# An eighth up-projection group in seven products, and low parts formed by accumulating DMAs

## The chip, the cores and the metric

The kernel runs on one core of one Trainium2 chip. The core has TensorE (PE in the profile, with PEld for its weight loads), VectorE (DVE), ScalarE (ACT), GpSimd (POOL) and SyncE (SP); SP and POOL issue the DMAs here. Each engine works through its own list of instructions in order and waits on semaphores of the others. The metric is the device time of one execution in microseconds (us); lower is better.

## The reference

Two layers of an encoder over 512 tokens with 1024 channels. Each layer has four mixing branches (a convolution module, neighbourhood attention, dilated attention, windowed attention) behind one input projection, merged by gates and projected back; then a ConvFFN:

```python
def _conv_ffn(h, w_up, conv_w, conv_b, w_down):
    u = _depthwise_conv(h @ w_up, conv_w, conv_b)
    gate, up = jnp.split(u, 2, axis=-1)
    return (jax.nn.silu(gate) * up) @ w_down
...
        x = x + mixed @ w_out[l]

        x = x + _conv_ffn(_rmsnorm(x, g_ffn[l]), w_up[l], ffn_conv_w[l], ffn_conv_b[l], w_down[l])
```

All is float32. `w_up` is 1024 x 5632 (2816 gate columns and 2816 up columns), `w_down` is 2816 x 1024, the depthwise convolution has width 3 along the tokens. The change lies in the ConvFFN alone.

## The kernel before

**Precision.** TensorE multiplies float32r, a float32 rounded to fewer bits. Each operand is split into a high part, hi = round(w), and a low part, lo = w - hi, and a product is three matmuls: hi x hi, hi x lo, lo x hi (L294 to L296, `prod`). So each weight tile of 128 x 1024 is loaded by SP into `w_raw` (L269), copied to `w_hi` by ACT (L273), and subtracted into `w_lo` by DVE (L275). A list, `w_list`, holds the weights of the whole program in the order of their use; `weights` emits each two units ahead of its use and with a high priority. `w_raw` has two buffers, `w_hi` and `w_lo` have three, so the parts of one unit can be written once TensorE has finished the unit three places earlier.

**Up-projection.** The 5632 columns are 44 blocks of 128: for i = 0 to 21 a gate block (s = 0) and an up block (s = 1). A block is 8 inner steps of three matmuls over all 512 tokens, 24 matmuls of 512 columns (`block`). Two neighbouring i make a group of four blocks; there are 11 groups. Groups 1 to 7 (`SEVEN`) are not made block by block. Each is one 2 x 2 block product (rows: gate and up; columns: the two halves of the 512 tokens; inner: even and odd steps of 128 channels) done by Winograd's scheme with seven products in place of eight: A11, S3, A22, S2, A12, S1, S4. One product is a unit of 24 matmuls of 256 columns (`seven`, L1128). The token side of the sums is formed once a layer (`ffn_form`). The weight side of the sums is formed in the raw tile: four quarters are loaded (L1270), and after the split of one unit a DMA from POOL's queue adds the next quarter onto the same tile (`grow`, L1258), which makes the next unit's weights. Each of these units is split into hi and lo by ACT (L1276) and DVE (L1277). Three of the seven results are copied out of PSUM by ACT (`sv`, L1140) and combined by DVE (L1143, L1147, L1152).

The list `UP_STEPS` sets the order: group 0 whole, then the units of the seven groups interleaved so that one group starts while the last one ends, then groups 8, 9 and 10 whole. Two blocks of the first whole group after them are drawn forward between the last units of seven products and kept in PSUM ("held" and "free").

**After each block.** DVE scales the result out of PSUM into a padded tile `U` (L1215, or L1144 to L1159 for seven products), which frees the PSUM bank. `conv_part` does the convolution in one ACT and two DVE operations (L1171 to L1173), ACT the silu for the gate half (L1177), DVE the product for the up half (L1185), which gives the activations f, kept two blocks to a tile of 128 x 1024.

**Down-projection.** It is a Winograd product as well, over 11 pairs of f blocks. Before its products a pair (f_i, f_k) has to become operands: DVE takes four sums of 256 columns (L1357, L1358, L1359, L1363), and f_i, f_k, the a-sums and the b-sum are each split into hi (ACT) and lo (DVE) at L1354 and L1355 (`split_pair`). Six pairs are split during the up-projection, after blocks 15 to 20 (`EARLY`), the five others in the first loop of `down`. The low parts are put into the tile of the f pair before (`pair_tags`), which is no longer needed then. The first products of `down` (L1376 to L1378) take four PSUM banks of the tag `mm`, which the last up blocks have used.

DVE, ACT and PE get their instructions in an order that a scheduler sets when the program is built, from the order of the code and its priorities.

Of the kernel before, what the change touches and what calls it, by code (L numbers as in the profile page):

```python
# [22 lines left out]
P = 128  # L23
L = 2
D = 1024
S = 512
KT = D // P
NB = S // P
DFF = 2816
# [3 lines left out]

CHUNK = 4

SEVEN = (1, 2, 3, 4, 5, 6, 7)


def up_steps():

    whole = lambda g: [('whole', 2 * g + i, s) for i in range(2) for s in range(2)]
    slots = {}
    for i, g in enumerate(SEVEN):
        for n, at in (('A11', 0), ('S3', 4), ('A22', 6), ('S2', 8), ('A12', 9), ('S1', 10), ('S4', 12)):
# [16 lines left out]
              ('gb', 'A22'), ('ga', 'S2'), ('ga', 'S1'), ('gb', 'S2'), ('gb', 'S1'), ('ga', 'S4'), ('gb', 'S4')]  # L61
MIX = (0, 1, 4, 5, 2, 3, 6, 7)

EARLY = (15, 16, 17, 18, 19, 20)
EPS = 1e-6
BIG = 1e30
EB = 4
# [167 lines left out]
class Trunk:  # L235
# [7 lines left out]
    def weights(self, upto, ahead=3000, parts=1, queue=None):  # L243

        nc = self.nc
        while self.w_emitted < min(upto, len(self.w_list)):
            n, pieces = self.w_list[self.w_emitted]
            if n == 'seven':
                with self.tc.high_priority(offset=ahead):
                    self.w_ready.append(self.seven_unit(*pieces))  # L250
                self.w_emitted += 1
                continue
            with self.tc.high_priority(offset=ahead):

                self.w_fast = (self.w_fast + 1) % 4 if n == 0 else 0
                if n == 0 and self.w_fast in (3, 0):
                    raw = self.fp.tile([P, 1024], F32, name="w_raw", tag="w_more", bufs=2)
                else:
                    raw = self.wpool.tile([P, 1024], F32, name="w_raw", tag="w_raw", bufs=2)
                hi = self.wpool.tile([P, 1024], F32R, name="w_hi", tag="w_hi", bufs=3)  # L260
                lo = self.wpool.tile([P, 1024], F32R, name="w_lo", tag="w_lo", bufs=3)
                src = pieces()
                n = sum(p.shape[1] for p in src)
                if len(src) == 1:
                    cut = [slice(i * n // parts, (i + 1) * n // parts) for i in range(parts)]
                    src = [src[0][:, s] for s in cut]
                c = 0
                for p in src:
                    (queue or nc.sync).dma_start(raw[:, c:c + p.shape[1]], p)  # L269
                    c += p.shape[1]  # L270
                for i in range(parts):
                    s = slice(i * n // parts, (i + 1) * n // parts)
                    w = nc.scalar.activation(hi[:, s], raw[:, s], AF.Copy)  # L273
                    self.first_hi = self.first_hi or w
                    nc.vector.tensor_tensor(lo[:, s], raw[:, s], hi[:, s].bitcast(F32), ALU.subtract)  # L275
            self.w_ready.append((hi, lo))
            self.w_emitted += 1

# [884 lines left out]
    def conv_part(self, i, s):  # L1163

        nc = self.nc
        v = nc.vector
        c = i + s * NF
        u = self.U[s][:, i % 2]
        y = self.fp.tile([P, S], F32, name=f"cy{s}", tag=f"cy{s}", bufs=2)
        w = lambda t: self.par('ffn_conv_w', c * 3 + t)  # L1170
        nc.scalar.activation(y, u[:, 1:513], AF.Identity, scale=w(1), bias=self.par('ffn_conv_b', c))  # L1171
        v.scalar_tensor_tensor(y, u[:, 0:512], w(0), y, ALU.mult, ALU.add)
        v.scalar_tensor_tensor(y, u[:, 2:514], w(2), y, ALU.mult, ALU.add)  # L1173

        if s == 0:
            si = self.fp.tile([P, S], F32, name="fth", tag="fth", bufs=2)
            nc.scalar.activation(si, y, AF.Silu)  # L1177
            self.silus[i] = si
            return
        if self.last and i % 2 == 1 and i // 2 < KT:  # L1180
            self.turn_res(i // 2)
        if i % 2 == 0:
            self.fpair = self.fp.tile([P, 1024], F32, name="f", tag=f"fp{i // 2}", bufs=1)
        fl = self.fpair[:, i % 2 * S:(i % 2 + 1) * S]
        v.tensor_tensor(fl, y, self.silus.pop(i), ALU.mult)  # L1185
        self.F.append(fl)
        if i in EARLY:
            self.split_pair(self.F, EARLY.index(i), self.got)

    def ffn(self, l, last):  # L1190
        nc = self.nc
        v = nc.vector
        self.U = []
        for i in range(2):
            u = self.conv_tile(f"U{i}")
            nc.gpsimd.memset(u[:, :, 0:1], 0.0)
            nc.gpsimd.memset(u[:, :, 513:514], 0.0)
            self.U.append(u)
        self.F, self.got, self.silus, self.sevens, self.last = [], {}, {}, {}, last
        held = {}  # L1200
        self.pace = 0.0
        for kind, a, b in UP_STEPS:
            if kind == 'seven':
                self.seven(a, b)
                continue
            if kind == 'free':
                ps = held.pop((a, b))
            else:
                ps = self.mm()
                self.block(ps)  # L1210
                self.tick()
            if kind == 'held':
                held[a, b] = ps
            else:
                v.tensor_tensor(self.U[b][:, a % 2, 1:513], ps, self.RB, ALU.mult)  # L1215
                self.conv_part(a, b)
        for g in self.slow:
            for _ in g:
                pass
        self.slow = []  # L1220
        return self.F
# [107 lines left out]
    def split_pair(self, F, j, got):  # L1329

        nc = self.nc
        v = nc.vector
        fi, fk = F[2 * j:2 * j + 2]

        def tile(t):
            if isinstance(t, tuple):
                t, n = t
                if n == 0:
                    pool = self.fp2 if t[:2] == "lt" else self.fp
                    self.halves[t] = pool.tile([P, 1024], F32R, name=f"p{t}", tag=t, bufs=1)  # L1340
                return self.halves[t][:, n * S:(n + 1) * S]
            pool = self.xpool if t[:2] in ("xh", "xl") else self.fp2 if t[:2] in ("fh", "t2", "t3") else self.fp
            return pool.tile([P, S], F32R, name=f"p{t}", tag=t, bufs=2 if t in ("lo", "xr", "xn", "cy0", "cy1") else 1)

        tags = self.pair_tags(j)
        ih, kh, il, kl, ah, al = (tile(t) for t in tags[:6])
        if j % 2 == 0:
            got['b'] = [tile(t) for t in tags[6:]]
        lo, hi = slice(0, 256), slice(256, 512)
        bh, bl = (t[:, (lo, hi)[j % 2]] for t in got['b'])  # L1350
        a = self.fp.tile([P, S], F32, name="sum", tag="xr" if j < len(EARLY) else "fth", bufs=2)

        def split(h, l, x):
            nc.scalar.activation(h, x, AF.Copy)  # L1354
            v.tensor_tensor(l, x, h.bitcast(F32), ALU.subtract)  # L1355

        v.tensor_tensor(a[:, lo], fi[:, hi], fk[:, hi], ALU.subtract)  # L1357
        v.tensor_tensor(fi[:, hi], fi[:, lo], fi[:, hi], ALU.subtract)  # L1358
        v.tensor_tensor(a[:, hi], a[:, lo], fi[:, lo], ALU.subtract)  # L1359
        split(ih, il, fi)  # L1360
        split(ah, al, a)
        split(kh, kl, fk)
        v.tensor_tensor(fk[:, lo], fk[:, lo], a[:, hi], ALU.add)  # L1363
        split(bh, bl, fk[:, lo])
        cut = lambda h, l, c: [(h[:, c + b * P:c + (b + 1) * P], l[:, c + b * P:c + (b + 1) * P]) for b in range(2)]
        got[j] = {'a11': cut(ih, il, 0), 's1': cut(ih, il, 256), 'a12': cut(kh, kl, 0), 's4': cut(kh, kl, 256),
                  's3': cut(ah, al, 0), 's2': cut(ah, al, 256), 'a22': cut(bh, bl, 0)}
# [108 lines left out]
    def run(self):  # L1476
        nc, tc = self.nc, self.tc
        with ExitStack() as st:
            pool = lambda name, **k: st.enter_context(tc.tile_pool(name=name, bufs=1, **k))
# [9 lines left out]
            for l in range(L):  # L1489
                off, quads, quarters, ups, mixing = 0, [], {}, {}, []  # L1490
                for kind, a, n in UNITS:
                    src = self.W[l, off:off + n * P].rearrange("(p c) -> p c", p=P)
# [16 lines left out]
                for kind, a, b in UP_STEPS:  # L1509
                    if kind == 'seven':  # L1510
                        self.w_list.append((kind, (l, a, b)))
                    elif kind != 'free':
                        self.w_list.append((1024, lambda src=ups[b * DFF + a * P]: [src]))
                self.quarters.append(quarters)
                self.quads.append(quads)
                self.sums.append([])
# [12 lines left out]
            with tc.tile_pool(name="first", bufs=1, reuse_waits="tile") as first:  # L1529
# [181 lines left out]
```

## Time and profile before

| | |
|---|---|
| three runs | 1549.47, 1544.78, 1548.46 us; median 1548.46 |
| the profiled execution, its own time | 1549.1 us |
| its span, first to last instruction | 1547.3 us |
| granted TensorE clock | 1.00 throughout |
| busy share of the span | PE 99%, PEld 86%, DVE 85%, ACT 62%, POOL 12% |
| DMA | 277.57 MB, 179 GB/s on average |
| layer 0: seven products, whole blocks, down-projection | about 447 to 610 us, 610 to 664 us, 664 to 760 us |
| layer 1: the same | about 1214 to 1382 us, 1382 to 1436 us, 1436 to 1530 us |

The busy time of an engine is the time in which at least one of its instructions ran. Matmuls overlap each other in TensorE's pipeline, so the cost of one is read from start to start. In a group of instructions, "out<-in" are the names of the tiles, then come the shapes, the count, the busy time of all, the mean duration of one in ns, and the idle time of the engine just before them with what ended it. Registers, branches and the issuing of DMAs don't count as busy. A wait names the instruction that waited and the one whose end released it. For a DMA the profile gives the time from its issue to its landing.

### The profile page before, as it was taken

To read this page: it belongs to the slowest core of one execution; us is meant where nothing else is said; L and a number is where in the kernel's file an instruction comes from. 1 tells how busy PE (TensorE), PEld (TensorE's weight loads), DVE (VectorE), ACT (ScalarE), POOL (GpSimd) and SP (SyncE) were. 2 spreads that over 40 slices of the span, in tenths; PEclk is the share of its full clock that TensorE was granted. 3 is DMA by queue.
4 is the path that set the end of the run, shared out by engine and by line. 5 is a ranking of instruction groups with operands and counts; after the bars stand their busy time and mean duration, and the time that the engine had idled before them with its cause. 6 is when DMAs were issued, how large, how long until landed. Compare 5 with 4: busy or idle time off the path is not lost.

```text
span 1547.3 us, 23306 instructions
## 1 busy us (share of the span) xinstructions
PE 1530.9 (99%) x8446; PEld 1325.7 (86%) x8446; DVE 1308.3 (85%) x2220; ACT 953.0 (62%) x1600; POOL 185.9 (12%) x280
## 2 busy tenths in 40 slices
PE   9999999999999999999999999999999999999998
PEld 8888888889889998878888888888898899998787
DVE  6689988797879989996576899887988789999974
ACT  6677777356655666564548687673566565665643
POOL 0123002220001110000002130023200011100000
PEclk9999999999999999999999999999999999999999
DMA  7789586756558886366558796866665699863664
GB/s 233 235 224 200 164 177 157 177 153 152 177 142 179 190 169 159 95 209 198 180 184 254 206 197 175 170 160 182 147 152 177 171 216 213 173 164 95 188 223 157
DMA packets 116739, 277.57 MB, mean 179 GB/s; under 512 B 27280, under 2 KB 29200, under 8 KB 116624
## 3 DMA queue, kind: packets, MB, share of 16 engines
q1 hardware_dynamic: 86800, 186.93, 37.7%
q0 software_dynamic: 29536, 88.62, 31.1%
q8 instruction: 67, 1.10, 0.3%
q10 hardware_dynamic: 288, 0.52, 0.1%
q14 instruction: 48, 0.39, 0.1%
HBM read 258.20 MB, written 58.72 MB: 205 GB/s over the span
## 4 chain that ended last, share of the span: by engine, by line
PE 69%; DVE 16%; DMA 6%; ACT 5%; issue 4%; SPq 0%; POOL 0%; ACTq 0%; DVEq 0%; POOLq 0%
PE mm L294 11%; PE mm L295 11%; PE mm L296 11%; PE aux L1128 5%; DVE w_lo L1277 4%; DMA chain<-W 4%; PE aux L948 3%; PE aux L1378 3%; PE aux L1377 3%; PE aux L1376 3%; DVE w_lo L275 2%; PE mm L1376 2%; PE mm L1378 2%; PE mm L1377 2%; DMA w_raw<-W 2%
## 5 line engine op out<-in xcount | busy, mean ns | idle before, releaser
L273 ACT ACTIVATE w_hi<-w_raw 128x1024 fp32r<-128x1024 f32 (+1 forms) x233 | 241.9, 1041 | 198.1 <-PE aux L1378 51.0
L275 DVE TENSOR_TENSOR w_lo<-w_raw,w_hi 128x1024 fp32r<-128x1024 f32 (+1 forms) x233 | 280.5, 1206 | 72.5 <-ACT w_hi L273 71.3
L294 PE MATMUL mm<-xh,w_hi 128*128 128x512 f32 x704 | 275.6, 391 | 0.0
L295 PE MATMUL mm<-xl,w_hi 128*128 128x512 f32 x704 | 274.6, 390 | 0.0
L296 PE MATMUL mm<-xh,w_lo 128*128 128x512 f32 x704 | 274.5, 390 | 0.0
L1128 PE MATMUL aux<-form,w_hi 128*128 128x256 f32 x896 | 160.8, 280 | 0.7 <-ACT sv L1140 0.7
L296 PEld LDWEIGHTS mm<-xh,w_lo 128*128 128x128 f32 x704 | 132.2, 188 | 28.3
L294 PEld LDWEIGHTS mm<-xh,w_hi 128*128 128x128 f32 x704 | 132.2, 188 | 26.3
L295 PEld LDWEIGHTS mm<-xl,w_hi 128*128 128x128 f32 x704 | 132.3, 188 | 25.9
L1128 PEld LDWEIGHTS aux<-form,w_hi 128*128 128x128 f32 x896 | 137.5, 188 | 1.7 <-ACT sv L1140 1.1
L1128 PE MATMUL aux<-form,w_lo 128*128 128x256 f32 x448 | 125.9, 281 | 0.0
L1277 DVE TENSOR_TENSOR w_lo<-chain,w_hi 128x1024 fp32r<-128x1024 f32 x72 | 87.9, 1220 | 32.2 <-ACT w_hi L1276 28.6
L1276 ACT ACTIVATE w_hi<-chain 128x1024 fp32r<-128x1024 f32 x72 | 76.0, 1056 | 61.4 <-DMA chain<-W 27.8
L469 DVE SCALAR_TENSOR_TENSOR cv<-cv,prm 128x512 f32<-128x512 f32 x120 | 94.7, 789 | 0.7
L1171 ACT ACTIVATE cy<-U,prm 128x512 f32<-128x512 f32 x88 | 67.9, 808 | 40.6 <-DVE U L1215 30.3
L1258 POOL DMA_DIRECT2D chain<-W x54 | 47.3, 876 | 328.9 <-DVE w_lo L1277 296.8
L1128 PEld LDWEIGHTS aux<-form,w_lo 128*128 128x128 f32 x448 | 84.1, 188 | 0.4 <-DVE w_lo L1277 0.4
L1276 ACT ACTIVATE w_hi<-w_raw 128x1024 fp32r<-128x1024 f32 x54 | 56.7, 1054 | 43.8 <-PE aux L1128 18.2
L532 PE MATMUL mm<-w_hi,xh 128*128 128x512 f32 x192 | 76.4, 398 | 0.3 <-DVE V L660 0.3
L533 PE MATMUL mm<-w_lo,xh 128*128 128x512 f32 x192 | 74.9, 390 | 0.0
L534 PE MATMUL mm<-w_hi,xl 128*128 128x512 f32 x192 | 74.9, 391 | 0.0
L1277 DVE TENSOR_TENSOR w_lo<-w_raw,w_hi 128x1024 fp32r<-128x1024 f32 x54 | 65.8, 1219 | 6.0 <-ACT w_hi L1276 4.6
(372 smaller groups left out, 3900.2 us busy)
## 6 DMA issues: line engine op xcount, KB each, us to landing
w_raw<-W SPq DMA_DIRECT2D x187, 512.0 KB, 4.4
chain<-W POOLq DMA_DIRECT2D x54, 512.0 KB, 5.7
sums<-W POOLq DMA_DIRECT2D x24, 1024.0 KB, 12.0
w_raw<-W SPq DMA_DIRECT2D x66, 256.0 KB, 3.8
w_raw<-sums SPq DMA_DIRECT2D x44, 256.0 KB, 3.8
w_raw<-sums SPq DMA_DIRECT2D x22, 512.0 KB, 4.3
sums<-W POOLq DMA_DIRECT2D x12, 768.0 KB, 10.3
chain<-W SPq DMA_DIRECT2D x18, 512.0 KB, 5.0
```

The costliest lines, as they stand in the source:

```text
L273: w = nc.scalar.activation(hi[:, s], raw[:, s], AF.Copy)
L275: nc.vector.tensor_tensor(lo[:, s], raw[:, s], hi[:, s].bitcast(F32), ALU.subtract)
L294: mm(ps, lhsT=wh, rhs=xh, start=start, stop=False)
L295: mm(ps, lhsT=wh, rhs=xl, start=False, stop=False)
L296: self.last_mm = mm(ps, lhsT=wl, rhs=xh, start=False, stop=stop)
L469: self.after_mm(v.scalar_tensor_tensor(acc, u[:, t:t + S], w(t), acc, ALU.mult, ALU.add))
L1128: self.last_mm = nc.tensor.matmul(o, lhsT=w[:, s], rhs=x, start=start and not (e or j or i), stop=j == 3 and i == 2, skip_group_check=True)
L1276: nc.scalar.activation(hi, raw, AF.Copy)
L1277: nc.vector.tensor_tensor(lo, raw, hi.bitcast(F32), ALU.subtract)
L1376: mm(ps, lhsT=x[0], rhs=w[0][:, cols], start=start, stop=False, skip_group_check=again)
L1377: mm(ps, lhsT=x[0], rhs=w[1][:, cols], start=False, stop=False, skip_group_check=again)
L1378: self.last_mm = mm(ps, lhsT=x[1], rhs=w[0][:, cols], start=False, stop=stop, skip_group_check=again)
```

## The change

**One more group in seven products.** `SEVEN` gets group 8. In each layer four whole blocks (16 and 17, gate and up) become seven units, and the held blocks are now those of block 18. The whole blocks after the seven groups are blocks 18 to 21.

**Six weights a layer get their low part by a DMA.** For the blocks 19, 20 and 21, both halves, ACT writes -hi into `w_lo` after it has written hi into `w_hi`, and a DMA from POOL's queue adds the weights onto it, a second time from DRAM: lo = -hi + w. The DVE subtraction goes.

**Six pairs get the low part of f by a DMA.** The early pairs are prepared by a new function, `early_pair`, now after the convolutions of blocks 17 (up), 19 (gate, up), 20 (gate, up) and 21 (gate). It makes the same sums on DVE; the two halves of f are copied as one 128 x 1024 tile by ACT (hi), ACT writes -hi, and a DMA from POOL's queue adds f onto it, from SBUF to SBUF. The a-sums and the b-sum are split as before. The five other pairs go through `split_pair` in `down` as before.

```diff
-SEVEN = (1, 2, 3, 4, 5, 6, 7)
+SEVEN = (1, 2, 3, 4, 5, 6, 7, 8)
...
-EARLY = (15, 16, 17, 18, 19, 20)
+EARLY = ((17, 1), (19, 0), (19, 1), (20, 0), (20, 1), (21, 0))
...
-                src = pieces()
+                src, summed = pieces(), n == 2
...
-                    nc.vector.tensor_tensor(lo[:, s], raw[:, s], hi[:, s].bitcast(F32), ALU.subtract)
+                    if summed:
+                        nc.scalar.activation(lo[:, s], hi[:, s].bitcast(F32), AF.Copy, scale=-1.0)
+                        nc.gpsimd.dma_start(lo[:, s], src[i], accum_op=ALU.add)
+                    else:
+                        nc.vector.tensor_tensor(lo[:, s], raw[:, s], hi[:, s].bitcast(F32), ALU.subtract)
...
-        if i in EARLY:
-            self.split_pair(self.F, EARLY.index(i), self.got)
+        if (i, 1) in EARLY:
+            self.early_pair(EARLY.index((i, 1)))
+
+    def early_pair(self, j):
...
+        f = self.fpairs[j]
...
+        hi = self.fp2.tile([P, 1024], F32R, name="pfh", tag=f"fh{j}", bufs=1)
+        low = self.fp.tile([P, 1024], F32R, name="plo", tag=f"fp{j - 1}" if j else "lo", bufs=1)
...
+        v.tensor_tensor(a[:, :256], q(1), q(3), ALU.subtract)
+        v.tensor_tensor(q(1), q(0), q(1), ALU.subtract)
+        nc.scalar.activation(hi, f, AF.Copy)
+        nc.scalar.activation(low, hi.bitcast(F32), AF.Copy, scale=-1.0)
+        nc.gpsimd.dma_start(low, f, accum_op=ALU.add)
+        v.tensor_tensor(a[:, 256:], a[:, :256], q(0), ALU.subtract)
...
+        v.tensor_tensor(b, q(2), a[:, 256:], ALU.add)
+        nc.scalar.activation(ah, a, AF.Copy)
+        v.tensor_tensor(al, a, ah.bitcast(F32), ALU.subtract)
+        nc.scalar.activation(bh, b, AF.Copy)
+        v.tensor_tensor(bl, b, bh.bitcast(F32), ALU.subtract)
...
-                        self.w_list.append((1024, lambda src=ups[b * DFF + a * P]: [src]))
+                        self.w_list.append((2 if a >= 19 else 1024, lambda src=ups[b * DFF + a * P]: [src]))
```

What stands in the engines' lists now, at three places. The first is POOL's queue of DMAs at the end of layer 0's up-projection. Before, the last addition onto a raw tile (`chain<-W`) is followed by nothing until the memsets of the next layer:

```order
L1258 DMA w_raw<-W 128x1024
L1258 DMA chain<-W 128x1024 x3
L1258 DMA w_raw<-W 128x1024
L1258 DMA chain<-W 128x1024
L441 MEMSET cv 128x15
L442 MEMSET cv 128x15
```

Now six additions onto low parts of weights (`w_lo`) and six onto low parts of pairs (`plo`) stand there, mixed:

```order
L1306 DMA chain<-W 128x1024
L277 DMA w_lo<-W 128x1024
L1215 DMA plo<-f 128x1024
L277 DMA w_lo<-W 128x1024 x2
L1215 DMA plo<-f 128x1024
L277 DMA w_lo<-W 128x1024 x2
L1215 DMA plo<-f 128x1024
L277 DMA w_lo<-W 128x1024
L1215 DMA plo<-f 128x1024 x3
L445 MEMSET cv 128x15
```

The queue is worked through in this order, so a weight's addition that stands behind a pair's is issued after it.

The second place is ACT's list around the last unit of seven products in layer 0 (`w_hi<-chain` is that unit's). Before, each `w_hi` is one row, and DVE does the rest; the pairs' copies (`pfh`, 512 wide) stand behind:

```order
L1276 ACTIVATE w_hi<-chain 128x1024
L273 ACTIVATE w_hi<-w_raw 128x1024
L1354 ACTIVATE pfh_6750<-f 128x512
L1354 ACTIVATE pfh_6751<-f 128x512
L1354 ACTIVATE pfh_6784<-f 128x512
L1354 ACTIVATE pfh_6785<-f 128x512
L1354 ACTIVATE pfh_6878<-f 128x512
L1171 ACTIVATE cy_6663<-U_4777,prm 128x512
L1171 ACTIVATE cy_6669<-U_4777,prm 128x512
```

Now `w_hi<-w_raw` is block 19's gate half, then its up half, and each has a negation into `w_lo`, with other operations between the two:

```order
L1324 ACTIVATE w_hi<-chain 128x1024
L273 ACTIVATE w_hi<-w_raw 128x1024
L1213 ACTIVATE pfh<-f 128x1024
L276 ACTIVATE w_lo<-w_hi 128x1024
L1175 ACTIVATE cy_6908<-U_4777,prm 128x512
L1175 ACTIVATE cy_6914<-U_4777,prm 128x512
L1214 ACTIVATE plo<-pfh 128x1024
L1219 ACTIVATE pe_6998<-sum 128x512
L273 ACTIVATE w_hi<-w_raw 128x1024
L1181 ACTIVATE fth<-cy_6908 128x512
L276 ACTIVATE w_lo<-w_hi 128x1024
```

A pair's copy now stands between the first weight's copy and its negation, and a silu between the second's.

The third place is DVE's list at the end of layer 0's up-projection, ahead of the evacuation of its last block into `U`, which frees a bank for the down-projection. Before, that is L1215, with splits of pairs (L1355) and a weight ahead of it:

```order
L1185 TENSOR_TENSOR f<-cy_7153,fth 128x512
L1358 TENSOR_TENSOR f<-f 128x256
L1359 TENSOR_TENSOR sum<-sum,f 128x256
L1355 TENSOR_TENSOR pfp_7161<-f,pfh_7160 128x512
L1355 TENSOR_TENSOR pfp_7161<-f,pfh_7159 128x512
L1355 TENSOR_TENSOR plt_7162<-sum,plt_7162 128x512
L1363 TENSOR_TENSOR f<-f,sum 128x256
L1215 TENSOR_TENSOR U_4777<-mm,RB 128x512
L275 TENSOR_TENSOR w_lo<-w_raw,w_hi 128x1024
L1355 TENSOR_TENSOR pe_7069<-f,pe_7068 128x256
L1172 SCALAR_TENSOR_TENSOR cy_7208<-U_4777,prm,cy_7208 128x512
L1215 TENSOR_TENSOR U_4780<-mm,RB 128x512
```

Now it is L1263; the two subtractions of f's halves are gone, and the splits of sums (L1220, L1222) wait for ACT:

```order
L1263 TENSOR_TENSOR U_4777<-mm,RB 128x512
L1218 TENSOR_TENSOR sum<-f,sum 128x256
L1220 TENSOR_TENSOR plt_7236<-sum,plt_7236 128x512
L1211 TENSOR_TENSOR sum<-f 128x256
L1222 TENSOR_TENSOR pe_7238<-sum,pe_7237 128x256
L1176 SCALAR_TENSOR_TENSOR cy_7285<-U_4777,prm,cy_7285 128x512
L279 TENSOR_TENSOR w_lo<-w_raw,w_hi 128x1024
L1177 SCALAR_TENSOR_TENSOR cy_7285<-U_4777,prm,cy_7285 128x512
L1212 TENSOR_TENSOR f<-f 128x256
L1216 TENSOR_TENSOR sum<-sum,f 128x256
L1263 TENSOR_TENSOR U_4780<-mm,RB 128x512
```

Between the last two evacuations stand nine rows where there were three, six more.

More of the change, by code (lines that the diff above doesn't have):

```diff
@@ L1178, in conv_part @@
             self.silus[i] = si
+            if (i, 0) in EARLY:
+                self.early_pair(EARLY.index((i, 0)))
             return
@@ L1183, in conv_part @@
             self.fpair = self.fp.tile([P, 1024], F32, name="f", tag=f"fp{i // 2}", bufs=1)
+            self.fpairs.append(self.fpair)
         fl = self.fpair[:, i % 2 * S:(i % 2 + 1) * S]
@@ L1186, in conv_part @@
         self.F.append(fl)
-        if i in EARLY:
-            self.split_pair(self.F, EARLY.index(i), self.got)
+        if (i, 1) in EARLY:
+            self.early_pair(EARLY.index((i, 1)))
+    def early_pair(self, j):
+        nc = self.nc
+        v = nc.vector
+        f = self.fpairs[j]
+        tags = self.pair_tags(j)
+        hi = self.fp2.tile([P, 1024], F32R, name="pfh", tag=f"fh{j}", bufs=1)
+        low = self.fp.tile([P, 1024], F32R, name="plo", tag=f"fp{j - 1}" if j else "lo", bufs=1)
+        ah, al = (self.pair_tile(t) for t in tags[4:6])
+        if j % 2 == 0:
+            self.got['b'] = [self.pair_tile(t) for t in tags[6:]]
+        bh, bl = (t[:, j % 2 * 256:j % 2 * 256 + 256] for t in self.got['b'])
+        a = self.fp.tile([P, S], F32, name="sum", tag="xr", bufs=2)
+        q = lambda n: f[:, n * 256:(n + 1) * 256]
+        v.tensor_tensor(a[:, :256], q(1), q(3), ALU.subtract)
[4 more added lines that the diff above has]
+        v.tensor_tensor(a[:, 256:], a[:, :256], q(0), ALU.subtract)
+        b = self.fp.tile([P, S], F32, name="sum", tag="xr", bufs=2)[:, :256]
+        v.tensor_tensor(b, q(2), a[:, 256:], ALU.add)
[3 more added lines that the diff above has]
+        v.tensor_tensor(bl, b, bh.bitcast(F32), ALU.subtract)
+        cut = lambda h, l, c: [(h[:, c + b * P:c + (b + 1) * P], l[:, c + b * P:c + (b + 1) * P]) for b in range(2)]
+        self.got[j] = {'a11': cut(hi, low, 0), 's1': cut(hi, low, 256), 'a12': cut(hi, low, 512),
+                       's4': cut(hi, low, 768), 's3': cut(ah, al, 0), 's2': cut(ah, al, 256), 'a22': cut(bh, bl, 0)}
@@ new lines, in pair_tile @@
+    def pair_tile(self, t):
+        if isinstance(t, tuple):
+            t, n = t
+            if n == 0:
+                pool = self.fp2 if t[:2] == "lt" else self.fp
+                self.halves[t] = pool.tile([P, 1024], F32R, name=f"p{t}", tag=t, bufs=1)
+            return self.halves[t][:, n * S:(n + 1) * S]
+        pool = self.xpool if t[:2] in ("xh", "xl") else self.fp2 if t[:2] in ("t2", "t3") else self.fp
+        return pool.tile([P, S], F32R, name=f"p{t}", tag=t, bufs=2 if t in ("xr", "xn", "cy0", "cy1") else 1)
@@ L1199, in ffn @@
         self.F, self.got, self.silus, self.sevens, self.last = [], {}, {}, {}, last
+        self.fpairs = []
         held = {}
@@ L1333, in split_pair @@
         fi, fk = F[2 * j:2 * j + 2]
[L1335 to L1343, printed above, removed]
+        tile = self.pair_tile
         tags = self.pair_tags(j)
```

## Prediction

> **What bounds the kernel now.** I read the busy shares first, then the table by stretches of the up-projection, then who waited for whom on PE, then single matmuls of PE in time order. The page and the table (columns: PE, PEld, DVE, ACT, POOL busy with the number of instructions, granted clock, DMA share, GB/s):
>
> ```profile
> span 1547.3 us, 23306 instructions
> PE 1530.9 (99%) x8446; PEld 1325.7 (86%) x8446; DVE 1308.3 (85%) x2220; ACT 953.0 (62%) x1600; POOL 185.9 (12%) x280
> ```
>
> ```profile
> 500.00:520.00 20.00, 20.00 (x170) 20.00 (x170) 19.70 (x26) 13.55 (x18) 3.51 (x4) 1.00 0.85 188
> ...
> 640.00:660.00 20.00, 20.00 (x90) 16.58 (x89) 19.96 (x34) 10.19 (x15) 0.00 (x0) 1.00 0.34 104
> ...
> 680.00:700.00 20.00, 20.00 (x87) 16.16 (x86) 19.94 (x36) 12.30 (x18) 0.00 (x0) 1.00 0.74 250
> ```
>
> 500 to 520 us lies in the groups that are made in seven products, 640 to 660 in the whole blocks, 680 to 700 in the down-projection, all of layer 0. PE is busy throughout at the full clock (1.00). DVE is full as well: 19.7, 19.96 and 19.94 us of 20. So the sum is made on PE, and DVE is the engine next behind it. How little PE loses to the others, its waits show:
>
> ```profile
> PE mm L1376 <- DVE U L1215: 1.1, 2, 0.8
> PE aux L1128 <- DVE w_lo L1277: 1.3, 3, 0.6
> PE aux L1128 <- ACT sv L1140: 0.7, 2, 0.5
> PE aux L1128 <- DVE sv L1152: 0.6, 2, 0.3
> ```
>
> The 14 groups in seven products (7 in each layer) cost 1.3 + 0.7 + 0.6 = 2.6 us of waiting, 0.19 us a group. The first row is the start of the down-projection: its first B product needs a PSUM bank that the last evacuation of the up-projection (L1215) still holds, since DVE runs behind. Nothing else of the stage waits, so at most 3.7 us can be had by feeding PE better. The rest must come from fewer or shorter matmuls.
>
> **The change part by part. Group 8 in seven products.** It removes 4 blocks of 24 matmuls of 512 columns and adds 7 units of 24 matmuls of 256, in each layer. A matmul's own duration (0.39 and 0.28 us) overlaps its neighbours, so I take the pace. In the 640 row 90 matmuls touch 20 us, of which 0.39/0.23 = 1.7 only reach in: 20/88.3 = 0.2265 us each. In the 500 row 170, less 2.4: 20/167.6 = 0.119 us. A whole group is 96 x 0.2265 = 21.7 us, a group of seven 168 x 0.119 = 20.0 us. That is 1.75 us a layer, **-3.5 us** for both. Single matmuls in time order say the same, eight steps of 0.227 and eight of 0.12:
>
> ```profile
> 442.28 0.39 PE L294 MATMUL mm<-xh,w_hi 128*128 128x512 f32 x1
> ...
> 444.10 0.39 PE L296 MATMUL mm<-xh,w_lo 128*128 128x512 f32 x1
> ...
> 448.37 0.28 PE L1128 MATMUL aux<-xh,w_hi 128*128 128x256 f32 x1
> ...
> 449.33 0.28 PE L1128 MATMUL aux<-xh,w_lo 128*128 128x256 f32 x1
> ```
>
> With 0.12 the gain is 1.58 us a layer, with 20/170 it is 1.98; -3.2 to -4.0 are the ends of this term.
>
> The new group brings the waits of its kind, 0.19 us in each layer: **+0.4 us** (0 to 1, if the second layer's groups are the dearer ones).
>
> **What it asks of DVE and ACT.** The rows of layer 0's stage, 440 to 760 us:
>
> ```profile
> L275 DVE TENSOR_TENSOR w_lo<-w_raw,w_hi 128x1024 fp32r<-128x1024 f32 x49 | 59.7, 1222 | 22.7 <-ACT w_hi L273 22.5
> ...
> L1143 DVE TENSOR_TENSOR sv<-aux,sv 128x512 f32<-128x512 f32 x7 | 4.8, 684 | 0.0
> ...
> L1355 DVE TENSOR_TENSOR pfp<-f,pxl 128x512 fp32r<-128x512 f32 x5 | 3.4, 685 | 0.0
> ```
>
> ```profile
> L273 ACT ACTIVATE w_hi<-w_raw 128x1024 fp32r<-128x1024 f32 x50 | 52.6, 1056 | 45.9 <-PE aux L1378 21.6 <-PE mm L1378 11.1 <-DMA w_raw<-W 3.6
> L1171 ACT ACTIVATE cy<-U,prm 128x512 f32<-128x512 f32 x44 | 34.0, 809 | 22.0 <-DVE U L1215 15.5 <-DVE U L1153 6.6
> ...
> L1177 ACT ACTIVATE fth<-cy 128x512 f32<-128x512 f32 x22 | 13.8, 626 | 6.7 <-DVE cy L1173 6.6
> L1140 ACT ACTIVATE sv<-aux 128x512 f32<-128x512 f32 x21 | 12.1, 577 | 2.3 <-PE aux L1128 2.3
> L1354 ACT ACTIVATE pfh<-f 128x512 fp32r<-128x512 f32 x12 | 7.0, 624 | 5.5 <-DVE f L1358 5.5
> ```
>
> DVE, a layer: group 8 adds 3 splits and 3 subtractions, 3 x 1.22 + 3 x 0.68 = 5.7 us. Six weight splits go (6 x 1.22 = 7.3) and twelve subtractions of pairs (12 x 0.685 = 8.2). That is 9.8 us less on a DVE with nothing to spare. ACT, a layer: 3 more w_hi and 3 sv (4.9), six negated weights (6.3), and for each pair one negation of 1.06 with one wide copy for two narrow ones (1.06 + 1.06 - 2 x 0.62, six times 5.2): 16.4 us more. ACT has 6 to 10 us idle in 20, so its sum is covered; its order is not, as shown next.
>
> **The six weights whose low part comes by an accumulating DMA** (both halves of blocks 19, 20 and 21). Before, a low part was ready 1.06 + 1.22 us after its buffer came free. Now it takes ACT's copy, ACT's negation and a DMA out of POOL's queue:
>
> ```profile
> w_raw<-W SPq DMA_DIRECT2D x187, 512.0 KB, 4.4
> chain<-W POOLq DMA_DIRECT2D x54, 512.0 KB, 5.7
> ...
> sums<-sums POOLq DMA_DIRECT2D x8, 1024.0 KB, 7.3
> ```
>
> ```profile
> 588.47 0.88 POOL L1258 DMA_DIRECT2D chain<-W  x1 [4.65 <-DVE w_lo L1277]
> 770.85 0.11 POOL L441 MEMSET cv<- 128x15 f32 x1 [181.51 <-DVE xn L1075]
> ```
>
> The chain's additions are the same transfer, 512 KB out of W onto SBUF: 5.7 us. POOL has nothing else there, 181 us idle. So 1.06 + 1.06 + 5.7 = 7.8 us. There are three buffers; one comes free when PE ends the unit three places earlier, and PE then has two units to run. For blocks 20 and 21 these are 2 x 5.44 = 10.9 us, and 3 us are left. For the first two weights one of the two units is group 8's S4, which runs only 24 x 0.119 = 2.9 us: 8.3 us. ACT's order puts a pair's wide copy (1.06) inside the first chain: 8.9, late by 0.6. The second weight's buffer comes free 5.44 us after the first's. By then ACT has the first chain's three operations, two cy, a pair's negation and its a-copy to do, 3 x 1.06 + 2 x 0.81 + 1.06 + 0.62 = 6.5 us, and comes 1.0 late; with one fth (0.63) inside the chain it is ready after 1.0 + 1.06 + 0.63 + 1.06 + 5.7 = 9.5 us, against 8.3 and the 0.6 that PE has lost by then: late by another 0.6. That is 1.2 a layer; ACT's operations overlap a little at their ends, while the first pair's transfer stands ahead in the queue. I take 0.8 us a layer, **+1.6 us** (0 to 4).
>
> The page "DMA: Bandwidth & Descriptors" of the Trainium skill, in its section "Anatomy of one DMA — SWDGE (gpsimd) path", prices such a transfer at 2.0 us plus its bytes over 436 GB/s, an estimate of 3.2 us for 512 KB. The 5.7 of the chain row is nearly twice that, so the measurement stands; by the page's price both weights would be in time and this term zero.
>
> **The six pairs.** Their low part is now -hi, with f added from SBUF to SBUF. No row shows that transfer. It is bounded by the plain load (4.4) and by an addition of twice the size that reads and writes DRAM (7.3); I take the chain's 5.7, the same bytes and the same kind of addition. The products that need these pairs are a stage away, so nobody on PE waits for it directly. But the low part lies in the buffer of the pair before, and ACT, which runs in order, cannot write it until that pair's transfer has landed. Behind it on ACT stand w_hi, cy and fth. Pairs come every 5.44 us, and 1.06 + 5.7 = 6.8 are needed: 1.3 us are lost a pair, some 5 over four pairs, against 9.8 that DVE won. So the wait at the start of the down-projection (1.1 us in all now) stays roughly: **-0.3 us** (-1.1 to +3).
>
> The extra 12 MB of DMA fall where the DMA share is 0.34; free. The sum: -3.5 + 0.4 + 1.6 - 0.3 = -1.8 us. The profiled execution took 1549.1 us, so 1547.3. It lies 0.6 above the median of the three runs (1548.46), which makes 1546.7 on their scale.
>
> **Rivals.** *The added latency is hidden.* ACT is idle for half of that stretch and may run ahead of my count; then no weight is late, and the lighter DVE ends the wait at the down-projection: -3.5 + 0.4 - 1.1 = -4.2, 1544.3 us. For it: the first weight misses by only 0.6 us in my count. Against: 5.7 is a median, and the second chain has another transfer ahead of it in its queue.
>
> *The pairs' transfers hold ACT up.* DVE's 9.8 us are used up when each of four pairs loses 2.45 us, at a landing of 5.44 - 1.06 + 2.45 = 6.8 us. From there ACT's delay reaches PE. At 7.3 the loss is 4 x 2.9 = 11.7: that is 1.9 us over, a wait of PE at the down-projection; each of the two late weights comes 1.6 later, and the 0.8 above stays: 5.9 us a layer, 11.8 in all. Beside -3.5 + 0.4 this makes +8.7, about 1557 us. For it: each pair's transfer has a weight's beside it in one queue, and the chain's own ones overlap too. Against: the source lies in SBUF, and the DMA share is low.
>
> *The weight loads become the bound.* Seven products need 168 loads for 96, and win only while one with its matmul costs under 96 x 0.2265 / 168 = 0.129 us. For it: PEld is busy for all of the 20 us at 500, and one load takes 188 ns; 896 of them fill 137.5 us with their overlaps counted once, 0.153 each:
>
> ```profile
> L1128 PEld LDWEIGHTS aux<-form,w_hi 128*128 128x128 f32 x896 | 137.5, 188 | 1.7 <-ACT sv L1140 1.1
> ```
>
> At that price a group takes 25.7 us, 4.0 a layer more than before: 1556 us. Against: the pace in that row of 500 is 0.119. The Trainium skill has a rule on this side too: "TensorE: Matmul & The Clock Gate", section "Back-to-back issue gap", gives a sustained spacing of 131 ns at 512 columns and 81 at 128, so by estimate 98 at 256: 16.4 us for seven products against 12.6, a loss of 3.9 a layer. The trace disagrees with it at both sizes, 0.2265 and 0.119.
>
> **How the numbers follow.** The likeliest case has 0.57 (1544 to 1550 by its terms), the hidden latency 0.28, the held-up ACT 0.13, the weight loads 0.02. Runs of this kernel lie up to 0.3% apart, so 0.3% (4.6 us) is about what can be told from no change: 1543.8 and 1553.1 are the edges. Faster: half of the second case and a seventh of the first, 0.22. Slower: nearly all of the last two, 0.14. Same: 0.64. The range 1542.5 to 1552 takes in the first two cases and leaves out most of the last two and the lowest edge.
>
> **What would show it.** Right: the windows of the added group show some 170 matmuls in 20 us; one PE wait of about a microsecond on a DMA into w_lo, at the second block half after group 8; DVE in the whole blocks below 18 of 20 us; additions into w_lo that land in about 5.7 us. Wrong: PE waits on w_lo at blocks 20 or 21; ACT idle until a DMA onto plo; a wait at the start of the down-projection of over 2 us; a landing of the pairs' transfers above 6.8 us; or PE's pace in group 8 above 0.129 us.

## The result, and the profile after

| | median us | runs | profiled execution | its span | clock |
|---|---|---|---|---|---|
| before | 1548.97 | 4 | 1549.1 | 1547.3 | 1.000 |
| after | 1562.31 | 4 | 1560.7 | 1559.0 | 0.998 |

The changed kernel takes 1.0091 times as long, with a 95% interval of 1.0066 to 1.0117: slower by 0.9%, some 13 us. The forecast was 1546.7 us, and its range ended at 1552.

The busy shares of the page after, to be held against the two rows of before:

```profile
span 1559.0 us, 23664 instructions
...
PE 1532.8 (98%) x8590; PEld 1331.8 (85%) x8590; DVE 1294.4 (83%) x2196; ACT 980.6 (63%) x1624; POOL 214.4 (14%) x312
```

The span grew by 11.7 us, PE's busy time by only 1.9, although PE's matmuls are cheaper in sum: so PE stands idle or runs slowly. Who PE waits for, after (total us, times, longest):

```profile
PE mm L300 <- DMA w_lo<-W: 7.9, 3, 4.1
...
PE mm L1415 <- DVE U L1263: 2.5, 2, 1.3
...
PE aux L1132 <- DVE sv L1156: 2.1, 5, 0.8
...
PE aux L1132 <- ACT sv L1144: 0.4, 2, 0.2
...
PE aux L1132 <- DVE w_lo L1325: 0.3, 1, 0.3
```

The first row is new: three waits for a low part that an accumulating DMA makes, 7.9 us instead of the 1.6 in the forecast. The start of the down-projection went from 1.1 to 2.5 us. The groups in seven products (the last three rows) wait about as long as before, 2.8 us against 2.6.

The longest of the three waits, as single matmuls of layer 1's block 19 (start, duration, and in brackets the idle time and who ended it):

```profile
1413.96 0.39 PE L298 MATMUL mm<-xh,w_hi 128*128 128x512 f32 x1
1414.19 0.39 PE L299 MATMUL mm<-xl,w_hi 128*128 128x512 f32 x1
1418.67 0.70 PE L300 MATMUL mm<-xh,w_lo 128*128 128x512 f32 x1 [4.09 <-DMA w_lo<-W]
1419.17 0.63 PE L298 MATMUL mm<-xh,w_hi 128*128 128x512 f32 x1
1419.60 0.63 PE L299 MATMUL mm<-xl,w_hi 128*128 128x512 f32 x1
...
1422.42 0.39 PE L300 MATMUL mm<-xh,w_lo 128*128 128x512 f32 x1
1422.64 0.39 PE L298 MATMUL mm<-xh,w_hi 128*128 128x512 f32 x1
```

All three waits lie in block 19, none in blocks 20 and 21. Behind this one the matmuls stand 0.43 us apart instead of 0.23, for some 3.5 us. The table by stretches gives the cause in the column of the granted clock, 0.52 and 0.51 (the two columns behind it are the DMA share and GB/s):

```profile
640.40:643.60 3.20, 3.20 (x9) 2.50 (x9) 2.89 (x5) 1.51 (x3) 0.36 (x1) 0.52 1.07 275
1418.70:1422.00 3.30, 3.30 (x8) 2.65 (x9) 3.30 (x6) 0.63 (x2) 0.00 (x0) 0.51 1.06 287
```

The same stretches of before:

```profile
640.40:643.60 3.20, 3.20 (x16) 2.64 (x15) 3.20 (x7) 0.60 (x2) 0.00 (x0) 1.00 0.50 120
1418.70:1422.00 3.30, 3.30 (x16) 2.72 (x15) 3.29 (x6) 2.47 (x3) 0.00 (x0) 1.00 0.56 164
```

PE counts as busy for all of both stretches, but at half the clock it runs eight or nine matmuls where it ran sixteen before. It costs 1.4 us in layer 0 and 1.7 in layer 1.

A ledger of the 11.7 us: steps between matmuls above the regular pace at the waits for w_lo, 1.75 + 2.43 + 0.29 + 4.26 = 8.7 (the 0.29 is a fourth, short delay, at the first weight of layer 1's block 19); half clock 3.1; the start of the down-projection 1.4 more; the predicted -3.1 for group 8. That makes 10.1. Of the 1.6 left, 0.9 is already there when layer 0's first unit of seven products starts (447.4 us instead of 446.5), ahead of everything that the change touches there; the rest I can't place.

Why the low parts come late, from the DMA part of the page (KB each, median us from issue to landing) and from the instructions of each line:

```profile
w_lo<-W POOLq DMA_DIRECT2D x12, 512.0 KB, 7.9
plo<-f POOLq DMA_DIRECT2D x12, 512.0 KB, 6.0
...
DMA to landing us min/median/max: 5.7/7.9/10.9
...
DMA to landing us min/median/max: 4.7/6.0/8.7
```

The first range is the weights', the second the pairs'. The 5.7 us of the forecast is the fastest of the twelve weights. In block 19 the second weight lands after 9.6 us in layer 0 and 10.0 in layer 1, while the first pair's transfer, the next weight's and two plain loads are under way.

### The profile page after: what moved, and what is told of

It is laid out like the page before. It is cut to its first block, busy times and chain, and to the rows that moved or that the text cites. A ratio compares the mean times of both kernels' runs of the same rounds, so it can differ in the third digit from the quotient of the medians.

```text
span 1559.0 us, 23664 instructions
## 1 busy us (share of the span) xinstructions
PE 1532.8 (98%) x8590; PEld 1331.8 (85%) x8590; DVE 1294.4 (83%) x2196; ACT 980.6 (63%) x1624; POOL 214.4 (14%) x312
## 4 chain that ended last, share of the span: by engine, by line
PE 74%; DVE 11%; DMA 5%; ACT 5%; issue 4%; SPq 0%; POOL 0%; DVEq 0%; ACTq 0%; POOLq 0%
PE aux L1132 11%; PE mm L298 10%; PE mm L299 10%; PE mm L300 10%; PE aux L952 3%; DVE w_lo L1325 3%; PE aux L1417 3%; PE aux L1416 2%; PE aux L1415 2%; DMA plo<-f 2%; PE mm L1415 2%; PE mm L1417 2%; PE mm L1416 2%; PE mm L1132 2%; PE mm L536 2%
## 5 line engine op out<-in xcount | busy, mean ns | idle before, releaser
L279 DVE TENSOR_TENSOR w_lo<-w_raw,w_hi 128x1024 fp32r<-128x1024 f32 (+1 forms) x213 | 256.1, 1205 | 70.2 <-ACT w_hi L273 68.3
L300 PE MATMUL mm<-xh,w_lo 128*128 128x512 f32 x640 | 251.4, 393 | 8.1 <-DMA w_lo<-W 7.9
L298 PE MATMUL mm<-xh,w_hi 128*128 128x512 f32 x640 | 252.0, 394 | 0.0
L299 PE MATMUL mm<-xl,w_hi 128*128 128x512 f32 x640 | 251.1, 392 | 0.0
L1132 PE MATMUL aux<-form,w_hi 128*128 128x256 f32 x1024 | 183.7, 280 | 0.5 <-ACT sv L1144 0.4
L1132 PEld LDWEIGHTS aux<-form,w_hi 128*128 128x128 f32 x1024 | 157.2, 188 | 1.4 <-ACT sv L1144 1.1
L300 PEld LDWEIGHTS mm<-xh,w_lo 128*128 128x128 f32 x640 | 120.9, 189 | 35.7 <-DMA w_lo<-W 9.8
L1132 PE MATMUL aux<-form,w_lo 128*128 128x256 f32 x512 | 144.2, 282 | 0.0
L1132 PEld LDWEIGHTS aux<-form,w_lo 128*128 128x128 f32 x512 | 96.1, 188 | 0.7 <-DVE w_lo L1325 0.6
L1132 PE MATMUL aux<-xh,w_hi 128*128 128x256 f32 x256 | 72.9, 285 | 2.1 <-DVE sv L1156 2.1
```

The lines of the kernel that those rows point to most:

```text
L298: mm(ps, lhsT=wh, rhs=xh, start=start, stop=False)
L299: mm(ps, lhsT=wh, rhs=xl, start=False, stop=False)
L300: self.last_mm = mm(ps, lhsT=wl, rhs=xh, start=False, stop=stop)
L1132: self.last_mm = nc.tensor.matmul(o, lhsT=w[:, s], rhs=x, start=start and not (e or j or i), stop=j == 3 and i == 2, skip_group_check=True)
```

## The experiments

The theories. **A**: the accumulations pile up. Weights' and pairs' transfers together stretch each other's landings, and PE waits in block 19. **B**: the chain of one weight (high part, negation, issue, landing) is too long by itself. **C**: group 8 in seven products costs more than it saves. A second reading of A came up on the way: **the chain over the pairs' buffers**, where the negation for pair j writes the buffer that the transfer of pair j - 1 still reads, the same chain as in the second rival. All ratios are to runs of the kernel before on the same chip.

| kernel | median us | ratio to before, 95% |
|---|---|---|
| weights by DMA, pairs by DVE | 1548.79 | 1.0008 (0.9996 to 1.0021) |
| pairs by DMA, weights by DVE | 1554.53 | 1.0046 (1.0032 to 1.0061) |
| group 8 alone, no accumulation | 1549.55 | 1.0007 (0.9998 to 1.0017) |
| whole change, high parts first | 1565.90 | 1.0118 (1.0104 to 1.0132) |
| whole change, pairs' transfers cut to 64 KB | 1548.74 | 1.0003 (0.9988 to 1.0018) |
| pairs by DMA, other buffers | 1546.78 | 0.9981 (0.9968 to 0.9994) |
| whole change, high parts first, other buffers | 1552.21 | 1.0020 (1.0010 to 1.0029) |
| weights by DMA, high parts first | 1545.55 | 0.9982 (0.9972 to 0.9991) |
| whole change, other buffers | 1557.99 | 1.0062 (1.0047 to 1.0077) |
| weights by DMA, high parts first, groups 1 to 7 only | 1548.02 | 0.9997 (0.9988 to 1.0006) |

### Only the weights' transfers

```
-        nc.scalar.activation(low, hi.bitcast(F32), AF.Copy, scale=-1.0)
-        nc.gpsimd.dma_start(low, f, accum_op=ALU.add)
+        v.tensor_tensor(low, f, hi.bitcast(F32), ALU.subtract)
```

> The changed kernel with the six pairs' low parts made by VectorE again (0.12 of the accumulating transfers' two kinds is left: the six weights of a layer stay with the DMAs). Theory A (the accumulations pile up: a weight's load, its accumulation and a pair's accumulation ask for more DMA time per block than TensorE gives them, so that a landing of 5 us alone grows to 7 to 10): with the pairs' transfers gone, landings of w_lo fall to 5 to 7 us, TensorE's waits for w_lo fall from 7.9 us to under 2.5, no stretch at half clock follows, and the time falls by 6 to 11 us of the 13 lost, to 1551 to 1556 us, unless VectorE, which gets 1.2 us a pair back, is late itself. Theory B (the chain of one weight - high part, negation, issue, landing - is too long for a look-ahead of two in block 19, whatever else is under way): the waits stay above 5 us in all, and the time above 1558 us.

Of the 24 accumulating transfers twelve are left here (not "0.12"). The loss is gone. PE's waits, and the landings of the weights:

```profile
PE mm L300 <- DMA w_lo<-W: 2.6, 2, 1.4
...
DMA to landing us min/median/max: 5.7/7.2/7.8
```

The waits, both for the first weight of block 19, are near the forecast's 1.6 and far below the 5 us that B asked for: B as the cause of the loss falls. The landings stay above 7 us as a median, but none is above 7.8: the second weight of block 19 now takes 7.3 and 7.7 us. What went is the tail. The time is better than A had said.

### Only the pairs' transfers

```
-                        self.w_list.append((2 if a >= 19 else 1024, lambda src=ups[b * DFF + a * P]: [src]))
+                        self.w_list.append((1024, lambda src=ups[b * DFF + a * P]: [src]))
```

> The changed kernel with the low parts of all up-projection weights made by VectorE again; the pairs' stay with the DMAs. Theories A and B alike: no wait for w_lo on a DMA, no stretch at half clock, landings of the pairs about 5 us, and a time of 1545 to 1550 us, about as before the change, since VectorE gets back 7.2 us a layer of weights. Theory C (the seventh-product group itself costs more on the engines than the 3.5 us that it saves on TensorE): still 1554 us or more, with waits of TensorE on VectorE's weights in the last blocks. If the pairs' own transfers hold the start of the down-projection up, the wait there is above 2 us in two.

Slower by 0.46%, which A had not expected: the pairs' transfers cost something with no weight beside them, as the last sentence had it. The number is also the one that C gave, but C's sign is missing: in the last blocks PE does not wait for VectorE's weights. PE's waits and ScalarE's wait for the pairs, over the whole run:

```profile
PE mm L1415 <- DVE U L1263: 6.5, 2, 3.5
```

```profile
ACT plo L1214 <- DMA plo<-f: 7.6, 6, 1.7
```

Both waits of PE stand at the start of the down-projection, 3.0 and 3.5 us, and a stretch at half clock follows each, which costs 1.4 and 1.6 us. ScalarE loses 1.3 us a wait, six times in the two layers, though a pair here lands in 4.8 us as a median.

### Group 8 alone

Both edits together.

> Only group 8 in seven products: both kinds of low parts are VectorE's again. By TensorE's own sum it is 3.5 us faster than before, 1545 us. VectorE was busy for all but a few tenths of a us between 618 and 664 us of the kernel before, and a group in seven products gives it three more weights' low parts of 1.2 us and three more operations of 0.68 on products, some 5.7 us a layer: if none of that is hidden, the start of the down-projection comes 5 us later in each layer, and the time is 1553 to 1557 us. Theory A and B say nothing against either; Theory C says 1555 us or more.

Neither number came out: it is as fast as before. The start of the down-projection now has two kinds of waits that before had not:

```profile
PE mm L1414 <- ACT w_hi L273: 2.4, 2, 1.2
...
PE aux L1415 <- DVE w_lo L279: 1.1, 2, 0.6
```

That is 3.5 us at this place against 1.1 before, and the groups in seven products wait 4.0 us in all against 2.6: 3.8 us more, about what the new group saves. Of the 5.7 us a layer that VectorE gets, PE sees the smaller part. C in its strong form falls: by itself the group costs nothing, and gains nothing either.

### High parts first

In blocks 19 to 21:

```
+            for k in range(KT):
+                mm(ps, lhsT=hi[:, s], rhs=self.Xh[k], start=k == 0, stop=False)
+                self.last_mm = mm(ps, lhsT=hi[:, s], rhs=self.Xl[k], start=False, stop=False)
...
+            for k in range(KT):
+                self.last_mm = mm(ps, lhsT=lo[:, s], rhs=self.Xh[k], start=False, stop=k == KT - 1)
```

> The changed kernel with all accumulating transfers, but in blocks 19 to 21 the sixteen matmuls on the high part of a weight come ahead of the eight on its low part, so that w_lo is wanted 16 x 0.2265 = 3.6 us later. If lateness of w_lo is what costs (A and B alike), waits of 1.6, 2.3, 0.3 and 4.3 us leave at most 0.7 us, no idle stretch is long enough for the half clock, and the time is 1547 to 1552 us. If the DMAs are saturated over all of blocks 19 to 21 (A in its strong form: the backlog only moves), waits of 2 us or more come back in blocks 20 and 21 or at the start of the down-projection, and the time stays above 1555 us.

The waits for w_lo are nearly gone, and the kernel is no faster: 1.0118 against 1.0091, with intervals that overlap. Time and place are those of the second alternative, waits of over 2 us at the start of the down-projection. PE's waits, then VectorE's around layer 0's last blocks, then ScalarE and GpSimd in order of time:

```profile
PE mm L1427 <- DVE U L1275: 10.6, 4, 3.7
...
PE mm L329 <- DMA w_lo<-W: 1.4, 2, 1.2
```

```profile
DVE pe L1232 <- ACT pe L1231: 5.1, 1, 5.1
```

```profile
646.54 1.04 ACT L276 ACTIVATE w_lo<-w_hi 128x1024 fp32r<-128x1024 f32 x1
651.66 1.06 ACT L1226 ACTIVATE plo<-pfh 128x1024 fp32r<-128x1024 f32 x1 [4.08 <-DMA plo<-f]
652.63 0.61 ACT L1231 ACTIVATE pe<-sum 128x512 fp32r<-128x512 f32 x1
```

```profile
642.35 0.87 POOL L277 DMA_DIRECT2D w_lo<-W  x1 [4.57 <-ACT w_lo L276]
643.15 0.97 POOL L1227 DMA_DIRECT2D plo<-f  x1
```

Read upward from PE: PE waits for the last evacuation of the up-projection on VectorE; VectorE stood 5.1 us for ScalarE's copy of a pair's sum (L1231); ScalarE stood 4.08 us ahead of that copy, in the negation (L1226), until the transfer of the pair before had landed. That transfer took 8.4 us, from 643.15 to 651.6. At the 4.7 us that the second pair's takes in the kernel with only the pairs' transfers, ScalarE's wait would have been some 0.3 us, an estimate from these rows. So the chain and the stretched landing are both in it.

The edit did more than it was meant to do: the scheduler also set ScalarE's and VectorE's lists in another order, and in GpSimd's queue the second pair's transfer now stands right behind the fifth weight's, where in the changed kernel it stood between the third's and the fourth's. That in the changed kernel the waits for w_lo hid this chain, because ScalarE's lateness costs nothing while PE waits in block 19, is therefore likely, but not shown by this run.

### Other buffers for the pairs' low parts

The low part of pair j goes where pair j - 2 stood; pair 1's goes into a new buffer that is otherwise only used late in the down-projection. `pair_tags` follows the same rule for the later pairs, and the order of the lists of ScalarE and VectorE changes only in the down-projections and just behind them; both hold for all three kernels below.

```
-        low = self.fp.tile([P, 1024], F32R, name="plo", tag=f"fp{j - 1}" if j else "lo", bufs=1)
+        low = (self.fp2 if j == 1 else self.fp).tile([P, 1024], F32R, name="plo", tag=("lo", "lt5")[j] if j < 2 else f"fp{j - 2}",
+                                                     bufs=1)
...
-        lo = ["lo", "lo"] if j == 0 else [(f"fp{j - 1}", 0), (f"fp{j - 1}", 1)]
+        lo = ["lo", "lo"] if j == 0 else [(f"fp{j - 2}", 0), (f"fp{j - 2}", 1)]
...
```

With the pairs' transfers alone:

> The kernel with only the pairs' transfers (1554.5 us), but the low part of pair j goes where the products of pair j - 2 stood (pair 1's into another buffer), so that ScalarE's negation for a pair no longer writes what the transfer of the pair before it still reads. If that chain of transfer, negation, transfer is the cause of the late start of the down-projection: no wait of ScalarE for a pair's transfer, the start's waits fall from 3.2 and 3.6 us to 1.5 or less, no half clock behind them, and 1547 to 1550 us. If the load of ScalarE and VectorE is the cause: waits at the start above 2.5 us, and 1553 us or more.

The chain is shown: ScalarE no longer waits for a pair, PE's only wait at the down-projection's start is 0.5 us, and the kernel goes from 1.0046 to 0.9981, a gain of 0.65% by that edit: faster than before.

With the high parts first and all the transfers:

> The same buffers in the kernel with all transfers and the high parts' products first (1565.9 us). If the chain over the pairs' buffers is what made that one late at the start of the down-projection (ScalarE waited 5.5 us for pairs there): the start's waits of 3.4, 2.1, 3.9 and 2.2 us fall to 1.5 or less each, no half clock, and 1548 to 1553 us. If the DMAs are too full for all of these transfers (landings 7 to 10 us): waits of over 2 us remain somewhere, and the time is above 1557 us.

From 1.0118 to 1.0020, and no stretch at half clock is left: the first alternative. But the weights land in 5.6 to 11.0 us, and waits remain:

```profile
PE mm L329 <- DMA w_lo<-W: 2.6, 2, 1.4
...
PE mm L1428 <- DVE U L1276: 1.4, 1, 1.4
```

With the whole change in its own order:

> The whole change with the one edit of the buffers (a pair's low part no longer goes where the transfer of the pair before it reads), products in the changed kernel's own order. With the pairs' transfers alone that edit was worth 7.8 us. If the chain over the buffers is all of the loss: 1546 to 1550 us. If the weights' accumulations, which land in 7 to 10 us among the pairs', are a second part of their own: waits for w_lo of 4 us or more in all stay, with a stretch at half clock where one is above 1.9 us, and the time is 1552 to 1558 us.

The second theory's number: 1.0062. By the medians the chain was a third of the loss here (0.29 of 0.91%), but the two intervals overlap, so that its share is rough; the rest goes with the weights' waits among the pairs' bytes. Of two waits above 1.9 us one was followed by half a clock:

```profile
PE mm L300 <- DMA w_lo<-W: 5.6, 3, 2.7
...
DMA to landing us min/median/max: 5.7/7.9/9.0
```

### The pairs' bytes

```
-        nc.gpsimd.dma_start(low, f, accum_op=ALU.add)
+        nc.gpsimd.dma_start(low[:, :128], f[:, :128], accum_op=ALU.add)
```

> The changed kernel with each pair's accumulating transfer cut to its first 128 of 1024 columns (64 KB instead of 512 KB): seven eighths of a pair's low part are left unadded, so the output is not the reference's. The instructions, their order and every wait stay. If the bytes of the pairs' transfers are what costs (they stretch the weights' transfers, and hold up the next negation until they land): landings of w_lo at 5 to 7.5 us, its waits 3 us or less in all, no wait of ScalarE for a pair, no half clock, and 1546 to 1551 us, as with the pairs' low parts on VectorE (1548.8). If it is ScalarE's six negations of 1.05 us a layer, or GpSimd's queue standing at a pair's issue ahead of a weight's, the waits stay and the time is 1556 us or more.

With every instruction of ScalarE, VectorE and GpSimd in its old order, and only seven eighths of the pairs' bytes left out, the loss goes too, and ScalarE waits for no pair; one wait of 1.9 us stays, with a half clock behind it that was not expected. PE's wait, and the landings of the weights and of the pairs:

```profile
PE mm L300 <- DMA w_lo<-W: 1.9, 1, 1.9
...
DMA to landing us min/median/max: 5.4/6.5/7.5
...
DMA to landing us min/median/max: 2.8/3.4/6.0
```

So neither ScalarE's negations nor GpSimd's queue is the cause by itself. The DMA share (the last column but one) is no guide here: from 630 to 640 us this kernel shows 0.98, the first row below, and the changed kernel 1.01.

```profile
630.00:640.00 10.00, 9.90 (x47) 7.71 (x47) 8.84 (x16) 9.95 (x13) 2.62 (x3) 1.00 0.98 220
```

```profile
630.00:640.00 10.00, 6.37 (x27) 4.92 (x28) 7.62 (x13) 8.44 (x12) 2.46 (x4) 1.00 1.01 241
640.00:650.00 10.00, 10.00 (x38) 8.10 (x37) 6.37 (x12) 5.75 (x9) 1.64 (x2) 0.83 0.86 208
650.00:660.00 10.00, 10.00 (x45) 8.27 (x45) 7.66 (x14) 7.67 (x10) 1.75 (x2) 1.00 0.94 193
```

### Weights by DMA, high parts first, and the group by itself

The edits of "Only the weights' transfers" and of "High parts first" together:

> The kernel with only the weights' transfers (1548.8 us), with the high parts' products first: its two waits for w_lo of 1.4 and 1.2 us lie within the 3.6 us by which w_lo is wanted later. If nothing is late behind them: 1545.5 to 1547.5 us, which would be faster than before by up to 0.15%. If they hid another lateness (VectorE's at the start of the down-projection): 1548 to 1550 us as it was.

As expected, and with no wait for w_lo left: faster than before by 0.18%, the lowest time of the study, level with the pairs' transfers in other buffers (0.19%). From here the group itself can be priced:

```
-SEVEN = (1, 2, 3, 4, 5, 6, 7, 8)
+SEVEN = (1, 2, 3, 4, 5, 6, 7)
```

> The fastest kernel so far with the weights' transfers (1545.6 us), but group 8 as four whole products again (groups 1 to 7 in seven). The term of the prediction for the group alone, 3.5 us on TensorE less 0.4 of waits: 1548.7 us. If the waits of the stage in seven products eat that gain (VectorE's results come 0.4 to 0.5 us late in most groups of the second layer): 1545 to 1546.5 us.

From 0.9982 to 0.9997, 0.15% of 1549: group 8 in seven products is worth 2.3 us where nothing new is late. The intervals of the two ratios overlap, so the size is rough.

## Why the prediction was wrong, by its steps

**The group, -3.5 + 0.4: near.** The kernels with and without it differ by 2.3 us against 3.1, with overlapping intervals. C is out as the cause of the loss.

**The weights, +1.6 (0 to 4): the place was right, the size failed.** The waits are in block 19, at both halves, and not in blocks 20 and 21, as worked out there. Alone, the weights' transfers cause 2.6 us of waits, within the bounds. In the changed kernel they cause 8.7. The step that failed took the landing of one row, 5.7 us, as a constant, and closed with "The extra 12 MB of DMA fall where the DMA share is 0.34; free". The new transfers do not spread over that stretch: by the working itself two weights, the first pair and the plain loads of the next weights fall within 8 us. There the second and third weights land after 9.3 to 10.9 us, and the DMA share, which was 0.34 without the new transfers, is 0.86 to 1.01. The weights were issued early enough: in layer 0 the second one was wanted 7.2 us after its issue, in layer 1 5.75 us. Had every weight of block 19 landed in 5.7 us, the same issues would have cost some 0.5 us of waits in both layers (an estimate from the times of the four issues and of the matmuls that waited), in place of 8.7. With seven eighths of the pairs' bytes left out the landings are 5.4 to 7.5, and the loss is gone.

**The pairs, -0.3 (-1.1 to +3): the mechanism was right, the balance was not.** The text named the chain over the buffers and priced it at 1.3 us a pair; in the kernel with only the pairs' transfers ScalarE's measured waits are 7.6/6 = 1.3 us. It then set that against 9.8 us which VectorE wins. With the weights left on VectorE it wins only 8.2 - 5.7 = 2.5 us a layer, 2.7 less than four pairs' 5.2; PE's measured waits there are 3.0 and 3.5 us. ScalarE waited for three pairs a layer, not four, which is 3.8 us, so this balance gives the sign and not the size. In the whole change ScalarE waited only 2.3 us for pairs, probably because PE's own waits gave it time; with those waits taken away, and the order changed with them, PE's waits behind the chain were 10.6 us.

**The second rival, "the pairs' transfers hold ACT up", was half of what happened,** and had 0.13. Its text counted on a landing of 6.8 us as the point from which it decides. Landings of 6.8 and more occurred only for the first two pairs of a layer (8.5 and 6.8, 6.9 and 8.7); from then on it was 4.7 to 6.1. Its argument "the source lies in SBUF, and the DMA share is low" was the same error as the one above. Other buffers alone take about a third of the loss away, fewer bytes all of it.

**No step had the half clock.** PE's idle times were charged at their length. They cost 3.1 us more, since the clock falls behind the longer ones.

**The signs of "wrong".** Two appeared: ACT idle until a DMA onto plo, and a start of the down-projection above 2 us in all (2.5). A third showed in part: three of twelve pairs landed after more than 6.8 us. No wait for w_lo came at blocks 20 or 21, and PE's pace in group 8 was the forecast one. VectorE was relieved as forecast (14.0 of 20 us busy from 640 to 660, by the two stretches' 6.37 and 7.66; the first of them is partly at half clock), and nothing came of it, since it no longer was the engine that was last.

What stays open: whether the weights' landings stretch in the DMA engines or at the memory that they share with the pairs. A kernel whose pairs' transfers keep their bytes but move them at another time was not tried.

## What to carry to other kernels

Price a transfer at the landing it has beside the others that the change puts next to it, not at the median of a row from a quieter stretch, and list what is issued within one landing's time. Where an operation is moved to a DMA, look at which buffer its result goes to: if that is the source of the transfer before, the engine that prepares it waits in order for each landing. And when a wait is taken away and the time does not fall, look for a second lateness behind it, and for a change in the order of the lists, before giving the theory up: here the pairs' chain came out where the weights' waits had gone. The two kernels that beat before keep one kind of transfer only, with its own chain mended.

## What the runs showed of the hardware that was not expected

**Half clock after short idle times.** Behind the start of the program, every delay of PE of up to 1.85 us (a step between matmuls, less the regular pace) was followed by the full clock. Of twelve of 1.94 us or more, in the changed kernel and five of the experiments, eleven were followed within 1.7 us by 2.6 to 3.5 us in which matmuls stood nearly twice as far apart (0.427 us instead of 0.227 at 512 columns), at a cost of 1.2 to 1.7 us each; one of 2.27 us was not. (Before one of the eleven the clock had not yet come back from the delay ahead of it.) The shortest that was, in the kernel with only the weights' transfers:

```profile
619.00:623.50 4.50, 3.56 (x17) 3.57 (x18) 4.03 (x5) 1.83 (x3) 0.00 (x0) 0.64 0.58 185
```

The Trainium skill, "TensorE: Matmul & The Clock Gate", section "What's actually happening", says that the clock is halved after at least one idle window of some 3.4 us and comes back after one busy window. The half clock and its duration agree with the runs; the 3.4 us of idling do not, since 1.94 was enough.

**Accumulating transfers of 512 KB.** From SBUF to SBUF they took 4.6 to 4.8 us in the up-projection of the kernel with only the pairs' transfers (the first three pairs of each layer), with no other of their kind under way; the later ones there, issued after the start of the down-projection, took 4.8 to 8.3. From DRAM to SBUF the fastest weights of each kernel took 5.3 to 5.7. In the changed kernel, where three or four of the new transfers and plain loads overlap, the second and third weights took 9.3 to 10.9.
